# Attention of a two-block transformer kernel as a pipeline of four steps in a written order, with sixteen convolution taps by the scalar engine and accumulating DMA

## The chip, the cores and the metric

The kernel runs on one core of a Trainium2 chip. The metric is the device time of one execution in microseconds (us), as the median of several runs. Engines are named as in the profile: PE is TensorE (matmul), PEld its weight loads, DVE the vector engine, ACT the scalar engine, POOL GpSimd, SP the sync engine, which issues most of the DMA.

## What is computed

Two blocks follow each other over 512 tokens of width 1024. The change lies in the second, whose mixer (in the reference) is

```python
h = rms_norm(x, norm1_g)
q, k, v, glu_a, glu_b = split(h @ w_in)        # 512 wide each, q, k, v in 8 heads of 64
q, k = rms_norm(q, q_norm_g), rms_norm(k, k_norm_g)     # per head
attn = stick_breaking_attention(q, k, v)

c = glu_a * sigmoid(glu_b)
c = causal_depthwise_conv(c, conv_dw_w) + conv_dw_b     # 31 taps, 512 channels
c = silu(layer_norm(c, conv_ln_g, conv_ln_b))
x = x + concat([attn, c]) @ w_out
```

and whose attention is, for each head, over strictly earlier tokens s < t:

```python
z = q @ k.T / sqrt(64)
log_beta, log_one_minus = log_sigmoid(z), log_sigmoid(-z)
tail[t, s] = sum of log_one_minus[t, j] over s < j < t
out = exp(log_beta + tail) @ v
```

A feed-forward layer with a three-tap convolution follows.

## The kernel before

Matmuls in fp32 accuracy are made of three in a reduced format: each operand is split into a hi and a lo part, and hi x hi, lo x hi and hi x lo are summed in PSUM (L127 to L129). Weights come from memory as units of 1 MB (`raw`) and are split on the way: the hi part `whi` by an ACT cast (L199), the lo part `wlo` by a DVE subtraction (L205), or, for some units of the second block, by an ACT pass (L202) and an accumulating DMA that POOL issues (L203).

In the second block the mixer goes in this order. `glu(i)` makes one of four 128-channel chunks of the gated product (L707). `heads` makes q, then k: for each of four token tiles a projection, an ACT square (L742), a DVE sum (L744), three POOL operations (L745 to L747) and a DVE product (L748), then transposes and a split (L144). `conv` issues the taps of the depthwise convolution: 30 taps of each chunk as a DVE scalar_tensor_tensor (L851) and one as an ACT activation with the bias. The list `TURNS` (L835) says which chunk is next. `project` makes the values (copied out of PSUM at L132).

Attention has 12 steps: four pairs of heads (hp), and three groups n of key blocks, of width `WIDE` 384, 384 and 512 for each of two heads. `sticks(hp, n)` (L775) makes the logits (L785) and the mask (L790) in a pair of PSUM banks, then the absolute value (L794 on ACT or L797 on DVE), exp and log (ACT L799, L800), the running total's summands (DVE L801), and splits them into hi (ACT copy L135) and lo (DVE L136). `breaks(hp, n)` (L804) adds the sums of the later keys on top of the logits by matmuls with fixed triangles of minus one (L814, L817) and takes the exponential, the weights, on ACT (L819). `gather(hp)` (L822) multiplies them with the values (L829) into a single bank and splits the result into the place of q.

PSUM has pairs of banks, of which three are free to attention at a time, and two single banks. `conv_norm` (L884) normalizes the convolution over channels: mean by matmuls with ones (L889), subtraction (L893), squares and their sums (L897), scale (L902 to L915), Silu (L917) and a split. `attended` (L949) multiplies the gathered heads with the output weights (`half_out`), scales the residual (L954) and adds (L957); the same is then done for the convolution's half.

Which instruction comes when on each engine is settled by a scheduler that models time, under the constraints of data and buffers; `tc.issue_after(x)` adds that an instruction is to come behind x on its engine. Before the change only the taps are bound so, through `tap` (L837).

Of the kernel before, what the change touches and what calls it, by code (L numbers as in the profile page):

```python
# [79 lines left out]
def block_kernel(  # L80
# [22 lines left out]
    def pair():  # L103
        return psp.tile([P, 2, 512], F32, tag="pp", name="pp")
# [663 lines left out]
    def cols_of(a):  # L768

        at = 256 if a == 3 else 0  # L770
        return slice(at, at + T - a * P)

    zs = {}

    def sticks(hp, n):  # L775

        w = WIDE[n]
        zt = pair()
        z = zt[:, :, :w]

        for i, (ks, qs) in enumerate(((kT[0], qT[0]), (kT[0], qT[1]), (kT[1], qT[0]))):
            for a in STEPS[n]:
                for e in range(2):
                    hs = slice(e * HD, (e + 1) * HD)
                    pe.matmul(z[:, e, cols_of(a)], ks[hs, hp, a * P : (a + 1) * P],  # L785
                              qs[hs, hp, a * P :], start=i == 0 and a < 3, stop=False,
                              skip_group_check=True)
        for a in STEPS[n]:
            for e in range(2):
                pe.matmul(z[:, e, cols_of(a)][:, :P], identr, never, start=False, stop=False,  # L790
                          skip_group_check=True)
        ex = v3(t4(), 2, w)
        if hp < 2:
            act.activation(ex, z, AF.Abs)  # L794
        else:

            dve.tensor_scalar(ex.bitcast(I32), z.bitcast(I32), 0x7FFFFFFF, None,  # L797
                              ALU.bitwise_and)
        act.activation(ex, ex, AF.Exp, scale=-1.0)  # L799
        act.activation(ex, ex, AF.Ln, bias=1.0)  # L800
        dve.scalar_tensor_tensor(ex, z, 0.0, ex, ALU.max, ALU.add)  # L801
        zs[hp, n] = z
        return copy_split(*blk(hp, n), ex)

    def breaks(hp, n):

        w = WIDE[n]
        z = zs.pop((hp, n))
        for e in range(2):
            for a in STEPS[n]:  # L810
                out = z[:, e, cols_of(a)]
                for b in range(a + 1, 4):
                    for s in blk(hp, 0 if b > 1 else 1):
                        pe.matmul(out[:, (b - a) * P :], negone, s[:, e, cols_of(b)], start=False,  # L814
                                  stop=False, skip_group_check=True)
                for i, s in enumerate(blk(hp, n)):
                    pe.matmul(out, negtri, s[:, e, cols_of(a)], start=False, stop=i == 1,  # L817
                              skip_group_check=True)
        return act.activation(taken(hp, n), z, AF.Exp)  # L819

    def gather(hp):

        o = single(0)
        for n in range(3):
            for a in reversed(STEPS[n]):
                for e in range(2):
                    hs = slice(e * HD, (e + 1) * HD)
                    vs = slice(hp * P + e * HD, hp * P + (e + 1) * HD)
                    pe.matmul(o[hs, a * P :], v2[:, a, vs], taken(hp, n)[:, e, cols_of(a)],  # L829
                              start=a == 3, stop=a == 0, skip_group_check=True)  # L830
        return copy_split(qT[0][:, hp, :], qT[1][:, hp, :], o)

    TURNS = [0] * 8 + [0, 1] * 22 + [1, 2] * 8 + [2, 3] * 22 + [3] * 8  # L835
    done = [0] * 4
    tap = None  # L837

# [14 lines left out]
                    ALU.mult, ALU.add)  # L853

    norm2 = half("D1", 4, T, F32)
    conv(8, glu(0))
    split_early(2)
    conv(16, glu(1))
    qT = heads("G", "qg", HD ** -0.5, (0, 4, 4, 8), lambda: conv(8, glu(2)), early[:2])
    kT = heads("F", "kg", 1.0, (0, 6, 5, 8), lambda: conv(12, glu(3)), early[2:])  # L860
    v2 = half("E0", 4, T, F32)
    stk = {}

    def place(i):
        if i not in stk:
            name = ("D0", "B0", "D1", "C0", "C1", "B1", "E1")[i]
            stk[i] = slot(name, F32R if i < 4 else F32)
        return stk[i]

    def blk(hp, n):  # L870

        tl = place((hp % 2, 2, 3)[n])
        return tuple(part(tl, 2, WIDE[n], 2 * WIDE[n] * i) for i in range(2))

    def taken(hp, n):

        at = (0, 1024 * (hp % 2), 768)[n]
        return part(place(6 if n == 1 else 4 + hp % 2), 2, WIDE[n], at)

    cl = None  # L880
    ch = []
# [89 lines left out]
    seq = [(hp, n) for hp in range(4) for n in range(3)]  # L971
# [144 lines left out]
```

## Time and profile before

| | |
|---|---|
| median of 3 runs | 1244.39 us (1243.74 to 1244.77) |
| profiled execution | 1245.94 us |
| its span | 1244.2 us |
| granted PE clock, mean of the span | 0.995 |
| PE busy | 1230.3 us, 5712 matmuls |
| DVE busy | 754.0 us |
| ACT busy | 495.0 us |
| POOL busy | 113.5 us |
| DMA | 126.71 MB, 102 GB/s in the mean |

An execution's own time is a little longer than the span between its first and last instruction. Busy times leave out waiting and the issuing of DMAs. In a timeline a row is a run of like instructions: start, time from the first start to the last end, engine, line, operation, output and input tile, count, and, in brackets, how long the engine had been idle before it and what ended that. Instructions on one engine overlap at their ends, so that the spacing of starts is shorter than the time of one. The line numbers are those of the kernel before.

### The profile page before, as it was taken

The numbers are of one execution on the slowest core, as the hardware profiler recorded it, in microseconds if no ns is written. First come the engines' busy times: TensorE is split into PE (matmuls) and PEld (weight loads), VectorE is DVE, ScalarE is ACT, GpSimd is POOL, SyncE is SP. The second block draws the span as 40 slices with busy tenths as digits, with TensorE's granted clock in tenths as the row PEclk, the third lists the DMA queues.
The fourth block names the chain that finished last, engine by engine and source line by source line (L and its number), as shares of the span: only waits on it lengthen the run. The fifth ranks groups of instructions, "written<-read, shape, count | busy, mean of one in ns | idle before, by whom it ended". The sixth has DMA issues, their size and how long they took to land.

```text
span 1244.2 us, 13667 instructions
## 1 busy us (share of the span) xinstructions
PE 1230.3 (99%) x5712; PEld 1014.1 (82%) x5712; DVE 754.0 (61%) x823; ACT 495.0 (40%) x534; POOL 113.5 (9%) x137
## 2 busy tenths in 40 slices
PE   9999999999999999999999999999999999999998
PEld 7889888788888888888888887667888888888887
DVE  7855634744766674466373899877575555346532
ACT  6433424623544342243255338764343333123310
POOL 1100210012000000000053440000400000000000
PEclk9999999999999999999999999899999999999999
DMA  7223222312222222222346254301322222222222
GB/s 274 101 104 132 102 102 68 136 68 98 73 100 102 102 102 102 88 85 99 119 152 169 68 130 104 106 1 68 102 102 82 89 100 102 102 102 102 84 70 83
DMA packets 21597, 126.71 MB, mean 102 GB/s; under 512 B 2336, under 2 KB 4256, under 8 KB 7840
## 3 DMA queue, kind: packets, MB, share of 16 engines
q1 hardware_dynamic: 20096, 117.20, 26.7%
q0 software_dynamic: 1152, 8.39, 3.5%
q8 instruction: 44, 0.72, 0.2%
q10 hardware_dynamic: 288, 0.26, 0.1%
q14 instruction: 17, 0.14, 0.0%
HBM read 115.35 MB, written 2.10 MB: 94 GB/s over the span
## 4 chain that ended last, share of the span: by engine, by line
PE 90%; DVE 4%; POOL 2%; ACT 2%; issue 1%; DMA 1%; SPq 0%; DVEq 0%; POOLq 0%; ACTq 0%
PE pp L129 27%; PE pp L127 27%; PE pp L128 27%; DVE H L851 2%; PE ps L128 1%; PE ps L129 1%; PE ps L127 1%; POOL col L746 1%; PE pp L814 1%; PE pp L817 1%; PE ps L829 1%; DMA wlo<-raw 1%; POOL col L745 1%; PE pp L785 0%; PE ps L326 0%
## 5 line engine op out<-in xcount | busy, mean ns | idle before, releaser
L199 ACT CAST whi<-raw 128x2048 fp32r<-128x2048 f32 (+3 forms) x109 | 197.9, 1817 | 415.5 <-PE pp L128 335.7
L129 PE MATMUL pp<-B,wlo 128*128 128x512 f32 x672 | 262.5, 391 | 0.2
L127 PE MATMUL pp<-B,whi 128*128 128x512 f32 x672 | 261.7, 390 | 0.8 <-ACT whi L199 0.7
L128 PE MATMUL pp<-C,whi 128*128 128x512 f32 x672 | 262.2, 390 | 0.0
L205 DVE TENSOR_TENSOR wlo<-raw,whi 128x2048 fp32r<-128x2048 f32 (+3 forms) x101 | 219.3, 2172 | 66.1 <-ACT whi L199 65.6
L128 PE MATMUL pp<-G,whi 128*128 128x512 f32 x448 | 175.0, 391 | 0.0
L129 PE MATMUL pp<-F,wlo 128*128 128x512 f32 x416 | 162.2, 390 | 0.0
L127 PE MATMUL pp<-F,whi 128*128 128x512 f32 x416 | 161.5, 389 | 0.0
L129 PEld LDWEIGHTS pp<-B,wlo 128*128 128x128 f32 x672 | 126.1, 188 | 28.2 <-DVE wlo L205 1.5
L127 PEld LDWEIGHTS pp<-B,whi 128*128 128x128 f32 x672 | 126.3, 188 | 28.0 <-ACT whi L199 1.7
L128 PEld LDWEIGHTS pp<-C,whi 128*128 128x128 f32 x672 | 126.2, 188 | 26.8 <-issue 0.5
L128 PEld LDWEIGHTS pp<-G,whi 128*128 128x128 f32 x448 | 84.1, 188 | 17.5 <-issue 0.2
L655 DVE SCALAR_TENSOR_TENSOR H<-H,sm,H 128x512 f32<-128x512 f32 x132 | 92.8, 746 | 0.7
L634 DVE TENSOR_TENSOR A<-pp,A 128x1024 f32<-128x1024 f32 x23 | 28.2, 1224 | 105.5 <-PE pp L129 105.5
L129 PEld LDWEIGHTS pp<-F,wlo 128*128 128x128 f32 x416 | 78.1, 188 | 16.5 <-issue 0.2
L127 PEld LDWEIGHTS pp<-F,whi 128*128 128x128 f32 x416 | 78.1, 188 | 16.4 <-issue 0.2
L851 DVE SCALAR_TENSOR_TENSOR H<-H,sm,H 128x512 f32<-128x512 f32 x120 | 83.2, 742 | 2.7 <-ACT H L132 2.5
L660 DVE TENSOR_TENSOR H<-pp,rb 128x1024 f32<-128x1024 f32 x22 | 26.8, 1224 | 50.6 <-PE pp L129 44.4
L132 ACT ACTIVATE H<-H,sm 128x512 f32<-128x512 f32 x70 | 54.3, 808 | 4.6 <-DVE H L707 4.6
L1010 DVE TENSOR_TENSOR H<-pp,rb 128x512 f32<-128x512 f32 x22 | 15.2, 691 | 60.4 <-PE pp L129 55.3
L127 PE MATMUL pp<-D,whi 128*128 128x512 f32 x112 | 43.6, 389 | 0.0
L128 PE MATMUL pp<-E,whi 128*128 128x512 f32 x112 | 43.6, 389 | 0.0
(315 smaller groups left out, 1826.3 us busy)
## 6 DMA issues: line engine op xcount, KB each, us to landing
raw<-in_wts SPq DMA_DIRECT2D x99, 1024.0 KB, 4.8
wlo<-raw POOLq DMA_DIRECT2D x8, 1024.0 KB, 7.0
raw<-in_wts SPq DMA_DIRECT2D x8, 768.0 KB, 4.2
A<-in_xT SPq DMA_DIRECT2D x3, 512.0 KB, 6.7
out<-A SPq DMA_DIRECT2D x3, 512.0 KB, 2.8
D<-in_memT SPq DMA_DIRECT2D x1, 1024.0 KB, 11.4
raw<-in_wts SPq DMA_DIRECT2D x3, 256.0 KB, 7.6
A<-in_xT SPq DMA_DIRECT2D x2, 256.0 KB, 3.9
```

Of the source, the lines that this page charges most:

```text
L127: pe.matmul(out, wh, xh, start=start, stop=False, **kw)
L128: pe.matmul(out, wh, xl, start=False, stop=False, **kw)
L129: pe.matmul(out, wl, xh, start=False, stop=stop, **kw)
L132: act.activation(out, in_, AF.Identity, scale=scale, bias=bias)
L199: act.copy(hi[:, cs], raw[:, cs])
L205: dve.tensor_tensor(lo[:, cs], raw[:, cs], hi[:, cs].bitcast(F32), ALU.subtract)
L634: dve.tensor_tensor(hu, pt, hu, ALU.add)
L655: dve.scalar_tensor_tensor(dst, hs[:, k : k + 512], w(k), dst, ALU.mult, ALU.add)
L660: dve.tensor_tensor(hs[:, :, 2:], pt, over2(rb), ALU.mult)
L745: pool.tensor_scalar(ms, ms, rr2[:, t : t + 1], EPS, ALU.mult, ALU.add)
L851: tap = dve.scalar_tensor_tensor(cv[:, i, :], cc[:, i, k : k + 512], par("dw_w", 4 * k + i), cv[:, i, :], ALU.mult, ALU.add)
L1010: dve.tensor_tensor(hs[:, 2:514], pt[:, 0, :], rb, ALU.mult)
```

## The change

Attention becomes a class `Step` with one object for each of the 12 steps, k = 3 hp + n. `put` binds every instruction of a step behind the one that was written before it for the same engine, so that the order on PE, ACT and DVE in the attention is the written one, taps included. Steps run four deep: logits(k+4), absolute(k+4), logs and total(k+3) and split(k+2) are issued around breaks(k). Steps with k % 4 == 3 use the two single banks, the others pairs. The gather writes into its own step's bank. The absolute value is on ACT for k < 4. The places of the split totals and of the weights in SBUF change.

Taps 22 to 29 of chunks 0 and 1, sixteen in all, are made on ACT as a scaled copy, and summed by 14 accumulating DMAs from POOL (256 KB each), each issued behind the power chain of a q or k tile; one DVE add puts the sum on top. `TURNS` has the other 104 taps. The core of the diff:

```diff
@@ heads
-            pool.tensor_scalar(ms, ms, rr[:, t : t + 1], None, ALU.mult)
+            power = pool.tensor_scalar(ms, ms, rr[:, t : t + 1], None, ALU.mult)
             conv(taps[t], dve.tensor_tensor(heads8, ...))
+            by_dma(power)
@@ attention
+    order = {}
+    def put(eng, op, *args, **kw):
+        with tc.issue_after(order[eng].ins) if eng in order else nullcontext():
+            order[eng] = op(*args, **kw)
+        return order[eng]
...
+        def logits(self):
+            hp, n, w = self.hp, self.n, self.w
+            if self.k % 4 < 3:
+                zt = pair()
+                self.z = [zt[:, e, :w] for e in range(2)]
+                self.all = [(slice(0, 2), zt[:, :, :w])]
+                self.bank = zt[:, 0, :]
+            else:
+                zt = [single(e) for e in range(2)]
+                self.z = [tl[:, :w] for tl in zt]
+                self.all = list(enumerate(self.z))
+                self.bank = zt[0]
...
+        def gather(self):
+            hp = self.hp
+            for n in range(3):
+                for a in reversed(STEPS[n]):
...
+                        put("pe", pe.matmul, self.bank[hs, a * P :], v2[:, a, vs],
+                            taken(hp, n)[:, e, cols_of(a)], start=a == 3, stop=a == 0,
+                            skip_group_check=True)
+        def keep(self):
+            hi, lo = qT[0][:, self.hp, :], qT[1][:, self.hp, :]
+            put("act", act.copy, hi, self.bank)
+            return put("dve", dve.tensor_tensor, lo, self.bank, hi.bitcast(F32), ALU.subtract)
@@ taps
-    TURNS = [0] * 8 + [0, 1] * 22 + [1, 2] * 8 + [2, 3] * 22 + [3] * 8
+    TURNS = [0] * 8 + [0, 1] * 14 + [1] * 8 + [2] * 26 + [2, 3] * 4 + [3] * 26
+    sums = half("D0", 4, T, F32)
+    aside = list(range(22, 30))
+    def by_dma(behind):
+        k = aside.pop(0)
+        for i in range(2):
+            out = sums[:, i, :] if k == 22 else sums[:, 2 + i, :]
+            act.activation(out, cc[:, i, k : k + 512], AF.Copy, scale=par("dw_w", 4 * k + i))
+            if k > 22:
+                with tc.issue_after(behind.ins):
+                    pool.dma_start(out=sums[:, i, :], in_=out, accum_op=ALU.add)
...
     v2 = half("E0", 4, T, F32)
+    dve.tensor_tensor(cv[:, 0:2, :], cv[:, 0:2, :], sums[:, 0:2, :], ALU.add)
@@ the loop
-    conv(10, sticks(*seq[0]))
-    conv(14, sticks(*seq[1]))
+    for k, n in ((0, 10), (1, 14)):
+        st = steps[k]
+        st.logits()
+        st.absolute()
+        st.logs()
+        st.total()
+        st.split()
+        taps_here(n)
     project()
-    todo = 2
-    for i, x in enumerate(seq):
-        while todo < len(seq) and todo <= i + 2 and not (x[1] == 2 and seq[todo][1] == 1):
-            conv(2, sticks(*seq[todo]))
-            todo += 1
-        weighted = breaks(*x)
-        if x[1] == 2:
-            gathered = gather(x[0])
+    for st in steps[2:4]:
+        st.logits()
+        st.absolute()
+    steps[2].logs()
+    steps[2].total()
+    for k, st in enumerate(steps):
+        a, b, c = (steps[k + i] if k + i < 12 else None for i in (4, 3, 2))
+        st.breaks()
+        weighted = st.weigh()
+        if b:
+            b.logs()
+        if st.n == 2:
+            st.gather()
+            gathered = st.keep()
+        if a:
+            a.logits()
+            a.absolute()
+        if b:
+            b.total()
+        if c:
+            c.split()
+        if TURNS:
+            taps_here(1 if k < 9 else 4)
```

`taps_here(n)` issues n taps behind the last DVE instruction of the chain.

The order of instructions at three places follows; L779 is `put` in the change, D_, B_ and C_ are places of split totals and weights, G_ and F_ the hi and lo parts of q and k, E_ weights or values, t_ work tiles, pp pairs and ps singles of PSUM, H_2138 the convolution's result, A_76 and A_77 the residual.

DVE at the entry of the attention, before. L801 is the total, the last of them here that of step 2:

```order
L707 TENSOR_TENSOR H_2137<-t_5003 128x512
L851 SCALAR_TENSOR_TENSOR H_2138<-H_2137,sm,H_2138 128x512 x10
L801 SCALAR_TENSOR_TENSOR t_5061<-pp,t_5061 128x768
L851 SCALAR_TENSOR_TENSOR H_2138<-H_2137,sm,H_2138 128x512
L801 SCALAR_TENSOR_TENSOR t_5088<-pp,t_5088 128x768
L851 SCALAR_TENSOR_TENSOR H_2138<-H_2137,sm,H_2138 128x512
L136 TENSOR_TENSOR D_5066<-t_5061,D_5066 128x768
L851 SCALAR_TENSOR_TENSOR H_2138<-H_2137,sm,H_2138 128x512 x2
L136 TENSOR_TENSOR D_5093<-t_5088,D_5093 128x768
L851 SCALAR_TENSOR_TENSOR H_2138<-H_2137,sm,H_2138 128x512 x2
L801 SCALAR_TENSOR_TENSOR t_5237<-pp,t_5237 128x1024
```

Between the product of L707 and total(2) there were 16 taps, in five groups. And now, on the same engine and from the same product; L779 with pp is total(0), total(1) and total(2) in turn, with D_ split(0) and split(1), L893 is the tap:

```order
L707 TENSOR_TENSOR H_2137<-t_5034 128x512
L893 SCALAR_TENSOR_TENSOR H_2138<-H_2137,sm,H_2138 128x512
L144 SCALAR_TENSOR_TENSOR F_4814<-pp,col_4804,F_4813 128x4x256
L893 SCALAR_TENSOR_TENSOR H_2138<-H_2137,sm,H_2138 128x512 x11
L779 SCALAR_TENSOR_TENSOR t_5093<-pp,t_5093 128x768
L893 SCALAR_TENSOR_TENSOR H_2138<-H_2137,sm,H_2138 128x512 x3
L779 TENSOR_TENSOR D_5098<-t_5093,D_5098 128x768
L893 SCALAR_TENSOR_TENSOR H_2138<-H_2137,sm,H_2138 128x512 x12
L779 SCALAR_TENSOR_TENSOR t_5120<-pp,t_5120 128x768
L779 TENSOR_TENSOR D_5125<-t_5120,D_5125 128x768
L893 SCALAR_TENSOR_TENSOR H_2138<-H_2137,sm,H_2138 128x512 x14
L779 SCALAR_TENSOR_TENSOR t_5269<-pp,t_5269 128x1024
```

Total(2) stood behind 10, 1, 1, 2 and 2 taps after the product of L707; it now stands behind 1, 11, 3, 12 and 14.

PE just behind the value projection, before (breaks(0), then breaks(1) and breaks(2)):

```order
L817 MATMUL pp<-D_5066,negtri 128x128 x2
L814 MATMUL pp<-D_5066,negone 128x256 x2
L814 MATMUL pp<-D_5066,negone 128x128 x2
L817 MATMUL pp<-D_5093,negtri 128x384 x2
L814 MATMUL pp<-D_5066,negone 128x256 x2
L814 MATMUL pp<-D_5066,negone 128x128 x2
L817 MATMUL pp<-D_5093,negtri 128x384 x2
L814 MATMUL pp<-D_5093,negone 128x384 x2
L814 MATMUL pp<-D_5066,negone 128x256 x2
L814 MATMUL pp<-D_5066,negone 128x128 x2
L889 MATMUL ps_5651<-H_2138,ones 128x512 x2
```

The breaks of the first three steps followed each other with no logits between. And now, on PE from the end of breaks(0):

```order
L779 MATMUL pp<-D_5098,negtri 128x128 x2
L779 MATMUL pp<-G_4553,F_4813 128x384 x2
L779 MATMUL pp<-G_4554,F_4813 128x384 x2
L779 MATMUL pp<-G_4553,F_4814 128x384 x2
L779 MATMUL pp<-never,identr 128x128 x2
L779 MATMUL pp<-D_5098,negone 128x256 x2
L779 MATMUL pp<-D_5098,negone 128x128 x2
L779 MATMUL pp<-D_5125,negtri 128x384 x2
L779 MATMUL pp<-D_5098,negone 128x256 x2
L779 MATMUL pp<-D_5098,negone 128x128 x2
L779 MATMUL pp<-D_5125,negtri 128x384 x2
L779 MATMUL pp<-G_4553,F_4813 128x512 x2
```

The logits of step 4 (384 wide) and of step 5 (512 wide) stand between breaks(0) and breaks(1) and between breaks(1) and breaks(2), in the PSUM pairs of steps 0 and 1.

DVE behind the last gather, before (L136 is the split of that gather, L893 the subtraction of the convolution's mean):

```order
L893 SCALAR_TENSOR_TENSOR H_2138<-ps_5651,H_2138 128x512 x4
L897 TENSOR_TENSOR t_5657<-t_5657,t_5660 128x512
L897 TENSOR_TENSOR t_5657<-t_5657,acc 128x512 x2
L906 TENSOR_SCALAR col_5676<-ps_5671 128x4
L908 TENSOR_TENSOR t_5678<-ident,col_5679 128x512
L136 TENSOR_TENSOR G_4553<-ps_5639,G_4552 128x512
L954 TENSOR_TENSOR A_76<-A_76,rb 128x1024 x2
L954 TENSOR_TENSOR A_77<-A_77,rb 128x1024 x2
L915 TENSOR_TENSOR H_2138<-H_2138,ps_5682 128x512 x4
```

Before, the mean was subtracted ahead of the split. And now on DVE (the first row is the split of the last gather; L1010 and L1013 are the old L954 and L957, L949 the old L893, L953 the old L897):

```order
L779 TENSOR_TENSOR G_4554<-ps_5569,G_4553 128x512
L1010 TENSOR_TENSOR A_76<-A_76,rb 128x1024 x2
L1010 TENSOR_TENSOR A_77<-A_77,rb 128x1024 x2
L949 SCALAR_TENSOR_TENSOR H_2138<-ps_5675,H_2138 128x512 x4
L1013 SCALAR_TENSOR_TENSOR A_76<-A_76,sm,pp 128x512 x2
L953 TENSOR_TENSOR t_5681<-t_5681,t_5684 128x512
L1013 SCALAR_TENSOR_TENSOR A_76<-A_76,sm,pp 128x512 x2
L205 TENSOR_TENSOR wlo<-raw,whi 128x2048
L953 TENSOR_TENSOR t_5681<-t_5681,acc 128x512 x2
L962 TENSOR_SCALAR col_5700<-ps_5695 128x4
L964 TENSOR_TENSOR t_5702<-ident,col_5703 128x512
```

The subtraction of the mean stood ahead of the last gather's split; it now stands behind it and behind the four products on the residual.

## Rows read from the trace of the kernel before

**Rows 1.** The page, section 1: busy us, share of the span, instructions of each engine

```profile
PE 1230.3 (99%) x5712; PEld 1014.1 (82%) x5712; DVE 754.0 (61%) x823; ACT 495.0 (40%) x534; POOL 113.5 (9%) x137
```

**Rows 2.** Windows, PE: stretch, us, busy (count), granted clock, DMA share, GB/s

```profile
785.00:790.00 5.00, 3.27 (x21) 0.93 0.93 375
790.00:800.00 10.00, 9.62 (x45) 0.52 0.01 2
800.00:830.00 30.00, 26.38 (x164) 1.00 0.00 1
830.00:855.00 25.00, 24.35 (x114) 1.00 0.00 1
```

**Rows 3.** Timeline of DVE, taps and totals ahead of the attention

```profile
690.53 3.10 DVE L851 SCALAR_TENSOR_TENSOR H<-H,sm,H 128x512 f32<-128x512 f32 x4
...
696.50 2.73 DVE L851 SCALAR_TENSOR_TENSOR H<-H,sm,H 128x512 f32<-128x512 f32 x4
...
753.35 0.68 DVE L707 TENSOR_TENSOR H<-t 128x512 f32<-128x512 f32 x1
...
768.14 1.21 DVE L801 SCALAR_TENSOR_TENSOR t<-pp,t 128x1024 f32<-128x1024 f32 x1
```

**Rows 4.** Timeline of ACT around the entry

```profile
765.72 1.06 ACT L800 ACTIVATE t<-t 128x1024 f32<-128x1024 f32 x1
...
769.83 1.92 ACT L202 ACTIVATE wlo<-raw 128x2048 fp32r<-128x2048 f32 x1 [1.80 <-PE ps L128]
...
773.45 1.04 ACT L135 CAST C<-t 128x1024 fp32r<-128x1024 f32 x1
...
776.21 0.66 ACT L132 ACTIVATE E<-ps,rr 128x512 f32<-128x512 f32 x1
...
778.57 0.81 ACT L819 ACTIVATE C<-pp 128x768 f32<-128x768 f32 x1
...
784.93 0.59 ACT L135 CAST G<-ps 128x512 fp32r<-128x512 f32 x1 [0.89 <-PE ps L829]
```

**Rows 5.** Timeline of PE around the entry

```profile
772.35 0.39 PE L129 MATMUL ps<-whi,C 128*128 128x512 f32 x1
772.58 0.33 PE L814 MATMUL pp<-D,negone 128*128 128x128 f32 x2
...
773.89 0.63 PE L814 MATMUL pp<-D,negone 128*128 128x256 f32 x4
...
775.57 0.94 PE L814 MATMUL pp<-D,negone 128*128 128x384 f32 x6
...
779.94 0.91 PE L785 MATMUL pp<-G,F 64*128 64x256 f32 x12
...
781.37 0.87 PE L829 MATMUL ps<-C,E 128*64 128x128 f32 x8
```

**Rows 6.** Timeline of PE in the loop, two waits for ACT

```profile
808.55 0.91 PE L785 MATMUL pp<-G,F 64*128 64x256 f32 x12 [0.90 <-ACT C L819]
...
820.54 1.08 PE L829 MATMUL ps<-C,E 128*64 128x512 f32 x4 [1.55 <-ACT C L819]
```

**Rows 7.** Timeline of DVE at the tail

```profile
832.42 2.48 DVE L893 SCALAR_TENSOR_TENSOR H<-ps,H 128x512 f32<-128x512 f32 x4 [0.51 <-PE ps L889]
...
843.38 4.62 DVE L954 TENSOR_TENSOR A<-A,rb 128x1024 f32<-128x1024 f32 x4
...
850.31 2.71 DVE L957 SCALAR_TENSOR_TENSOR A<-A,sm,pp 128x512 f32<-128x512 f32 x4
852.95 2.28 DVE L205 TENSOR_TENSOR wlo<-raw,whi 128x2048 fp32r<-128x2048 f32 x1
```

**Rows 8.** Line L203 on POOL, ns of one; the page's DMA issues, KB, us to landing

```profile
L203 POOL DMA_DIRECT2D wlo<-raw x8: 838/920/1047, 656.1 to 776.6; - x8
...
DMA to landing us min/median/max: 6.9/7.0/8.9
...
out<-A SPq DMA_DIRECT2D x3, 512.0 KB, 2.8
```

More of the change, by code (lines that the diff above doesn't have):

```diff
@@ L771, in cols_of, with __init__ @@
         return slice(at, at + T - a * P)
[L773 to L781, printed above, removed]
+    order = {}
[3 more added lines that the diff above has]
+        return order[eng]
+    class Step:
+        def __init__(self, k):
+            self.k, self.hp, self.n = k, k // 3, k % 3
+            self.w = WIDE[self.n]
+        def logits(self):
[10 more added lines that the diff above has]
+                self.bank = zt[0]
+            for i, (ks, qs) in enumerate(((kT[0], qT[0]), (kT[0], qT[1]), (kT[1], qT[0]))):
+                for a in STEPS[n]:
+                    for e in range(2):
+                        hs = slice(e * HD, (e + 1) * HD)
+                        put("pe", pe.matmul, self.z[e][:, cols_of(a)],
+                            ks[hs, hp, a * P : (a + 1) * P], qs[hs, hp, a * P :],
+                            start=i == 0 and a < 3, stop=False, skip_group_check=True)
@@ L782, in sticks @@
             for a in STEPS[n]:
                 for e in range(2):
[L784 to L788, printed above, removed]
-            for e in range(2):
-                pe.matmul(z[:, e, cols_of(a)][:, :P], identr, never, start=False, stop=False,
-                          skip_group_check=True)
@@ L792, in sticks @@
[L792 to L831, printed above, removed]
@@ L835, in block_kernel, with absolute @@
-    TURNS = [0] * 8 + [0, 1] * 22 + [1, 2] * 8 + [2, 3] * 22 + [3] * 8
+                    put("pe", pe.matmul, self.z[e][:, cols_of(a)][:, :P], identr, never,
+                        start=False, stop=False, skip_group_check=True)
+        def absolute(self):
+            self.ex = v3(t4(), 2, self.w)
+            for e, z in self.all:
+                if self.k < 4:
+                    put("act", act.activation, self.ex[:, e], z, AF.Abs)
+                else:
+                    put("dve", dve.tensor_scalar, self.ex[:, e].bitcast(I32), z.bitcast(I32),
+                        0x7FFFFFFF, None, ALU.bitwise_and)
@@ new lines, in logs, with total, split @@
+        def logs(self):
+            put("act", act.activation, self.ex, self.ex, AF.Exp, scale=-1.0)
+            put("act", act.activation, self.ex, self.ex, AF.Ln, bias=1.0)
+        def total(self):
+            for e, z in self.all:
+                put("dve", dve.scalar_tensor_tensor, self.ex[:, e], z, 0.0, self.ex[:, e],
+                    ALU.max, ALU.add)
+        def split(self):
+            hi, lo = blk(self.hp, self.n)
+            put("act", act.copy, hi, self.ex)
+            return put("dve", dve.tensor_tensor, lo, self.ex, hi.bitcast(F32), ALU.subtract)
@@ new lines, in breaks @@
+        def breaks(self):
+            hp, n = self.hp, self.n
+            for e in range(2):
+                for a in STEPS[n]:
+                    out = self.z[e][:, cols_of(a)]
+                    for b in range(a + 1, 4):
+                        for s in blk(hp, 0 if b > 1 else 1):
+                            put("pe", pe.matmul, out[:, (b - a) * P :], negone,
+                                s[:, e, cols_of(b)], start=False, stop=False,
+                                skip_group_check=True)
+                    for i, s in enumerate(blk(hp, n)):
+                        put("pe", pe.matmul, out, negtri, s[:, e, cols_of(a)], start=False,
+                            stop=i == 1, skip_group_check=True)
@@ new lines, in weigh @@
+        def weigh(self):
+            for e, z in self.all:
+                last = put("act", act.activation, taken(self.hp, self.n)[:, e], z, AF.Exp)
+            return last
+        def gather(self):
+            hp = self.hp
+            for n in range(3):
+                for a in reversed(STEPS[n]):
+                    for e in range(2):
+                        hs = slice(e * HD, (e + 1) * HD)
+                        vs = slice(hp * P + e * HD, hp * P + (e + 1) * HD)
+                        put("pe", pe.matmul, self.bank[hs, a * P :], v2[:, a, vs],
+                            taken(hp, n)[:, e, cols_of(a)], start=a == 3, stop=a == 0,
+                            skip_group_check=True)
@@ L865, in place @@
         if i not in stk:
-            name = ("D0", "B0", "D1", "C0", "C1", "B1", "E1")[i]
-            stk[i] = slot(name, F32R if i < 4 else F32)
+            name = ("D1", "B0", "D0", "B1", "C0", "C1", "E1")[i]
+            stk[i] = slot(name, F32R if i < 5 else F32)
         return stk[i]
     def blk(hp, n):
-        tl = place((hp % 2, 2, 3)[n])
+        tl = place((hp % 2, 2 + hp % 2, 4)[n])
         return tuple(part(tl, 2, WIDE[n], 2 * WIDE[n] * i) for i in range(2))
     def taken(hp, n):
-        at = (0, 1024 * (hp % 2), 768)[n]
-        return part(place(6 if n == 1 else 4 + hp % 2), 2, WIDE[n], at)
+        i, at = ((5 + hp % 2, 0), (6, 768), (5, 768))[n]
+        return part(place(i), 2, WIDE[n], at)
     cl = None
@@ L969, in project, with taps_here @@
             identity(v2[:, t, :], ps, scale=rr[:, t : t + 1])
-    seq = [(hp, n) for hp in range(4) for n in range(3)]
-    conv(10, sticks(*seq[0]))
-    conv(14, sticks(*seq[1]))
-    project()
-    todo = 2
-    for i, x in enumerate(seq):
-        while todo < len(seq) and todo <= i + 2 and not (x[1] == 2 and seq[todo][1] == 1):
-            conv(2, sticks(*seq[todo]))
-            todo += 1
-        weighted = breaks(*x)
-        if x[1] == 2:
-            gathered = gather(x[0])
+    steps = [Step(k) for k in range(12)]
+    def taps_here(n):
+        conv(n, order["dve"])
+        order["dve"] = tap
+    for k, n in ((0, 10), (1, 14)):
[6 more added lines that the diff above has]
+        taps_here(n)
+    project()
+    for st in steps[2:4]:
[21 more added lines that the diff above has]
+            taps_here(1 if k < 9 else 4)
     with tc.issue_after(weighted.ins):
```

## The prediction

> **What bounds the kernel now.** I read the busy shares first: TensorE (PE) is busy 99% of the span, the vector engine (DVE) 61%, the scalar engine (ACT) 40% [rows 1]. So the end is set by PE's work and by the gaps in it; work taken from DVE or ACT is worth nothing unless PE waited for it. Then I cut the attention stretch into windows [rows 2]. PE's gaps there are 5.00 − 3.27 = 1.73, 10.00 − 9.62 = 0.38, 30.00 − 26.38 = 3.62 and 25.00 − 24.35 = 0.65 us, together 6.4 us. The granted clock is 0.93 in the first window and 0.52 in the second, after those first gaps: that is the lower of PE's two levels (1.2 of 2.4 GHz) for nearly the whole window, and it cost about 9.62 x 0.48 + 3.27 x 0.07 = 4.8 us. The two together, **11.2 us, are all that a perfect order of the attention could give back**. PE's matmuls are the same before and after, so the forecast is a count of PE's waits: 11.2 us old ones against the new. Last I read each engine's timeline around 772 us, where the value projection ends and the attention loop begins (the entry), and around 842 us, where the last gather ends (the tail).
>
> **Taps moved off DVE.** Sixteen taps leave. A DVE tap that alternates between two tiles costs 2.73 / 4 = 0.68 by its group, 0.663 by spacing of starts; one that follows another on the same tile costs 3.10 / 4 = 0.775 [rows 3]. The saving is 16 x 0.663 = 10.6 us, less the one added add of some 0.7, less about 0.11 for every tap that the new order of chunks (26 twos in a row, 26 threes in a row) links to its predecessor: about 48 x 0.11 = 5.3. Some 4.6 us of DVE time are gained, on an engine that is busy 61% [rows 1]. The sixteen ACT passes are some 0.8 us each, 13 us on an engine with half its time free there: cost 0. POOL issues 14 accumulating DMAs at about 0.92 [rows 8], off PE's path: cost 0, the cover being the time until the single add behind the k heads. Landing time of a 256 KB accumulating transfer is not in the trace: 2.8 us (512 KB without accumulation) and 7.0 us (1 MB with it) [rows 8] bound it. I take 3.6, nearer the first since it is a quarter of the second's bytes: hidden. At 7.0 the chain of them could hold the add, and with it DVE, by up to 8 us; that end stays in the range.
>
> **The entry.** This term decides. Three things stand in fixed order now. PE: logits(3), breaks(0), logits(4), breaks(1), logits(5). Since logits(4) takes the PSUM pair of step 0, it needs the weights' Exp of step 0, and logits(5) that of step 1, which stands on ACT behind the hi copy of step 2, and that behind total(2) on DVE. PE gets there at 772.6, when the value projection ends [rows 5].
> - DVE: the gated product of chunk 3 ends at about 754 [rows 3]; behind it the change has 27 taps (18 linked x 0.775 + 9 x 0.663 = 19.9), the k heads' split (1.2) and total(0), split(0), total(1) at about 0.87 (384 columns a head against 1.21 for 512 [rows 3]): total(1) is done at 754 + 23.7 = 777.7.
> - ACT: four weight casts run from 769.83, two in 773.45 − 769.83 = 3.62 us, with the values' copy-out among them [rows 4]: free at 777.63. So copy(1) ends at 778.5 and split(1) at 779.4.
> - DVE then has 14 taps (10.7) ahead of total(2): 779.4 + 10.7 + 1.2 = 791.3. Copy(2) takes 1.04 and the Exp of step 1 0.81 [rows 4]: logits(5) may start at **793.2**. In the trace before, total(2) runs at 768.14, ahead of most of these taps [rows 3]. That is the step that moves: 14 taps now stand in front of an operation for which ACT, and through it PE, waits.
> - PE work meanwhile: logits(3) 781.37 − 779.94 = 1.43, breaks(0) 773.89 − 772.58 = 1.31, breaks(1) 775.57 − 773.89 = 1.68 [rows 5], logits(4) about 1.0 (six columns of 384 in place of twelve shorter matmuls): 5.4 us. New wait 793.2 − 772.6 − 5.4 = **15.2 us**, in three gaps: about 3.3 (logits(3) behind the copy-out that frees the single banks), 4.5 (logits(4)) and 7.4 (logits(5)).
>
> The row shows 3.10 us for four linked taps and 2.73 for four alternating ones [rows 3], so a dependence on the instruction just before costs 0.11 us. The Trainium skill (VectorE: DVE Perf Modes, section "The DRAIN you can't avoid") has it otherwise: a semaphore between successive operations costs nothing extra, since the pipe is drained in any case. By that rule total(2) would come with 30 linked taps at 0.663, some 3.4 us earlier on DVE alone; copy(1) would still wait for ACT, so logits(5) would start at about 791.7 and the sum would be 1.5 us less. The measurement decides, and I keep 0.775.
>
> **The loop.** After the entry each logits(k+4) follows breaks(k) and needs the Exp between them. The trace has one such wait: 0.90 us in front of an L785 group, released by ACT's L819 [rows 6]. For k = 3, 4, 6, 7 that is 3.6 us. For k = 2, 5, 8 the gather writes the very bank that this Exp reads, so it waits too: 1.55 was seen for a gather behind an Exp [rows 6], 0.9 is the least, and I take 1.1: 3.3. Behind the gathers at k = 2 and 5 logits(k+4) need the bank emptied: copy 0.59 [rows 4], subtract some 0.68, hand-over, 1.35 each: 2.7. **9.6, say 10 us.** Nothing stands on PE between that could cover it; before, the sums L889 and the other order did. Bounds: 0, if the scalar engine runs a step ahead, to 16, if every wait is 1.55.
>
> **The tail.** The convolution's mean needs a single bank, and step 11 holds both until its last Exp. So its four matmuls stand behind gather(11), where before they were spread over the loop and the subtraction L893 began at 832.42, ahead of the last gather [rows 7]. DVE's order is now: subtract of keep, four products of L1010 (4.62), the four subtractions (2.48), the first adds of L1013 (2.71), a weight's lo part 2.28 [rows 7] and three sums of squares (about 2.0), 15.4 with the 1.3 of the copy ahead. PE's cover is the mean's matmuls (1.8) and 23 products at 0.23 (772.35 to 772.58 [rows 5]): 7.0. Wait 8.4, and about 1 more where the first convolution product waits for the scale and the Silu: **9.4 us.** Bounds: 3, if the rotation of DVE's order lets the four subtractions pass, to 12.
>
> **Clock.** Two of the new groups of gaps, entry and tail, are longer than the 2.1 us of gaps after which the trace shows 0.52 [rows 2]. Each should cost what the one cost, 4.8: two come (9.6), the old one goes.
>
> **Sum.** New waits 15.2 + 10 + 9.4 = 34.6; old waits −6.4; clock 9.6 − 4.8 = +4.8. Together +33.0 on the profiled execution's 1245.94 us: 1278.9. That execution stands 1.5 us over the median of the runs, 1244.39, so the median forecast is **1277**.
>
> **Rivals.**
> - *Half clock in the loop as well* (0.13): gaps of one to two us come every 4 us from k = 2 on. For it: the old fall followed gaps of just this size. Against: 800 to 830 had 3.62 us of gaps in 30 and kept 1.00 [rows 2]. Price: three more episodes, +14: 1291.
> - *The accumulating DMAs land late* (0.10): at 7.0 us each the last taps' sum holds the add at the head of DVE's attention work: +8, 1285.
> - *Half the price* (0.12): the taps or casts at the entry run earlier than counted and the loop's waits overlap with one another: entry 8, loop 5, tail 5, one clock episode: 18 − 6.4 = +11.6: 1256.
> - *Faster* (0.10): with four steps in flight each operand is ready when PE comes to it. DVE reaches the 14 taps so early that total(2) is done by 778, 13 us ahead of my count; the entry then costs only the 3.3 of the copy-out, and the clock never falls. With 2 us of tail: 5.3 − 11.2 = −5.9, 1238.5. It decides from the point where all new waits with their clock are under 11.2 us. For it: 16 taps are off DVE before the entry. Against: ACT is bound by its casts until 777.6 whatever DVE does, and the taps stand ahead of total(2) in a written order.
> - *No change* (0.05): new waits equal the relief, or the moved taps and steps were never on PE's path, and the gaps are merely relocated: 1244.
>
> **How the numbers follow.** The forecast case has 0.50. Slower by more than 0.2% (2.5 us, about what a measurement of this kernel can tell from no change) hold the forecast, the first three rivals: 0.85; faster 0.10, same 0.05. The forecast case alone, with the bounds of loop and tail (−10 to +6, and −6 to +3, not all together), runs from 1264 to 1284. The range goes down to 1252, which takes in half the price, and up to 1297, which takes in the half clock; outside lie about 0.17 below and a few hundredths above.
>
> **What would show it.** Right: a PE gap of over 5 us ending at an L785-like logits group released by ACT's Exp around 790; a second window of granted clock near 0.5 behind it; 0.9 to 1.5 us in front of each logits group in the loop, released by the Exp; and a gap of some 8 us behind the last gather, released by the sums of squares. Wrong: total(2) done before 780, PE windows with gaps under 11 us in all, a mean that starts ahead of the last gather, or a wait of DVE for a transfer in front of the new add.

## The result and the profile after

| | before | changed |
|---|---|---|
| median | 1244.45 us (4 runs, 1243.74 to 1244.77) | 1285.84 us (4 runs, 1280.97 to 1286.17) |
| ratio | | 1.0324, 95% interval 1.0299 to 1.0349 |
| profiled execution, its span | 1245.94 us, 1244.2 us | 1280.97 us, 1279.3 us |
| granted clock of the span | 0.995 | 0.982 |

The change is slower by 3.2%; the forecast was 1277, in a range from 1252 to 1297. The profiled execution is the shortest of the four; the other three, at a granted clock of 0.977, are 5 us longer, about what one more fall of the clock costs, so times inside the trace are held against 1280.97 and medians against 1285.84.

The page's busy times, as [rows 1], say that PE did the same number of matmuls, with 97% of a longer span:

```profile
PE 1239.1 (97%) x5712; PEld 1021.5 (80%) x5712; DVE 752.6 (59%) x815; ACT 505.2 (39%) x552; POOL 125.0 (10%) x151
```

PE's windows, which answer to [rows 2], with the same columns; the stretches are the value projection, the entry, two pieces of the loop, its end with the products of the gathered heads, and the tail:

```profile
745.00:770.00 25.00, 19.62 (x86) 0.80 0.71 174
780.00:810.00 30.00, 18.22 (x97) 0.72 0.54 140
810.00:830.00 20.00, 14.95 (x112) 1.00 0.01 2
830.00:840.00 10.00, 8.94 (x44) 0.66 0.00 0
840.00:870.00 30.00, 28.89 (x152) 1.00 0.00 1
870.00:890.00 20.00, 13.90 (x48) 0.74 0.15 52
```

The reader is to see two things in each row: the gap (length less busy) and the clock. The gaps are 5.4, 11.8, 5.1, 1.1, 1.1 and 6.1, together 30.5 us. The clock cost 19.62 x 0.20 = 3.9, 18.22 x 0.28 = 5.1, 8.94 x 0.34 = 3.0 and 13.90 x 0.26 = 3.6: 15.6 us. That is 46.1 us in place of the old 11.2, or 34.9 more; the spans differ by 35.1. Nearly the whole loss is therefore in PE's waits between 745 and 890 and in the clock that fell after them.

What PE waited for between 640 and 900 (total, times, longest):

```profile
PE pp L779 <- ACT C L779: 7.6, 5, 3.3
PE pp L779 <- ACT E L779: 6.3, 2, 5.4
PE ps L958 <- DVE t L953: 6.1, 1, 6.1
PE ps L128 <- DMA wlo<-raw: 5.0, 2, 3.0
PE pp L779 <- DVE G L779: 2.8, 2, 1.4
PE ps L779 <- ACT E L132: 2.0, 1, 2.0
```

And where, in PE's timeline (in brackets the idle time before the row, and what ended it; L779 is `put`):

```profile
749.15 0.80 PE L128 MATMUL ps<-wlo,B 128*128 128x512 f32 x1 [2.00 <-DMA wlo<-raw]
...
760.12 0.79 PE L128 MATMUL ps<-wlo,B 128*128 128x512 f32 x1 [3.04 <-DMA wlo<-raw]
...
784.28 0.90 PE L779 MATMUL ps<-G,F 64*128 64x256 f32 x12 [1.98 <-ACT E L132]
...
791.21 1.33 PE L779 MATMUL pp<-G,F 64*128 64x384 f32 x6 [3.32 <-ACT C L779]
...
801.62 1.65 PE L779 MATMUL pp<-G,F 64*128 64x512 f32 x6 [5.37 <-ACT E L779]
...
819.88 0.96 PE L779 MATMUL pp<-G,F 64*128 64x512 f32 x6 [0.90 <-ACT E L779]
...
824.92 1.52 PE L779 MATMUL pp<-E,E 128*64 128x128 f32 x12 [1.11 <-ACT C L779]
...
828.71 0.91 PE L779 MATMUL pp<-G,F 64*128 64x256 f32 x12 [1.41 <-DVE G L779]
...
877.35 1.87 PE L958 MATMUL ps<-ones,t 128*128 128x1 f32 x8 [6.10 <-DVE t L953]
```

The rows at 784, 791 and 801 are logits(3), logits(4) and logits(5): the three gaps of the entry that were forecast, ended by the releasers that were named. Those at 819 to 828 are the loop's pattern: a weights' Exp, a gather behind its Exp, a bank that is emptied. The row at 877 is the tail. The first two rows were not forecast: PE waits for the lo parts of the value weights. POOL's timeline in front of them shows why (L909 issues the taps' DMAs, L203 the weights'):

```profile
738.98 1.84 POOL L909 DMA_DIRECT2D D<-D  x2 [0.15 <-issue]
740.29 1.41 POOL L203 DMA_DIRECT2D wlo<-raw  x1
...
745.15 1.85 POOL L909 DMA_DIRECT2D D<-D  x2 [0.17 <-issue]
748.62 0.86 POOL L203 DMA_DIRECT2D wlo<-raw  x1 [1.62 <-ACT wlo L202]
```

In the kernel before, the same two units were issued at

```profile
735.86 0.93 POOL L203 DMA_DIRECT2D wlo<-raw  x1 [0.53 <-ACT wlo L202]
...
748.60 0.94 POOL L203 DMA_DIRECT2D wlo<-raw  x1 [6.04 <-ACT wlo L202]
```

In the change each is issued behind a pair of tap transfers, but only the first is issued later than before, by 4.4 us: ACT makes its lo pass (L202) at 738.09 in place of 733.64, behind tap passes that waited for their own transfers. The second is issued at the same time as before, 748.62 for 748.60, so all its delay lies behind the issue. Landing, for the line L203, and on the page for both kinds:

```profile
DMA to landing us min/median/max: 6.9/7.8/11.5
...
wlo<-raw POOLq DMA_DIRECT2D x8, 1024.0 KB, 7.8
...
D<-D POOLq DMA_DIRECT2D x14, 256.0 KB, 3.8
```

The slowest weight unit took 11.5 us (the second of the two), where before the slowest took 8.9 and the median was 7.0 [rows 8].

### The profile page after: what moved, and what is told of

Same layout as the page of the kernel before. It is cut to its first block, busy times and chain, and to the rows that moved or that the text cites. A ratio compares the mean times of both kernels' runs of the same rounds, so it can differ in the third digit from the quotient of the medians.

```text
span 1279.3 us, 13713 instructions
## 1 busy us (share of the span) xinstructions
PE 1239.1 (97%) x5712; PEld 1021.5 (80%) x5712; DVE 752.6 (59%) x815; ACT 505.2 (39%) x552; POOL 125.0 (10%) x151
## 4 chain that ended last, share of the span: by engine, by line
PE 93%; DVE 2%; ACT 2%; DMA 1%; issue 1%; SPq 0%; DVEq 0%; ACTq 0%
PE pp L128 28%; PE pp L129 28%; PE pp L127 28%; PE pp L779 3%; PE ps L128 2%; PE ps L129 2%; PE ps L127 2%; PE ps L779 1%; DMA wlo<-raw 1%; DVE H L893 1%; PE ps L326 0%; ACT whi L199 0%; ACT C L779 0%; DMA A<-in_xT 0%; PE ps L345 0%
## 5 line engine op out<-in xcount | busy, mean ns | idle before, releaser
L655 DVE SCALAR_TENSOR_TENSOR H<-H,sm,H 128x512 f32<-128x512 f32 x132 | 92.8, 747 | 0.7
L893 DVE SCALAR_TENSOR_TENSOR H<-H,sm,H 128x512 f32<-128x512 f32 x104 | 75.8, 748 | 4.3 <-ACT H L132 2.5
L1090 DVE TENSOR_TENSOR H<-pp,rb 128x512 f32<-128x512 f32 x22 | 15.2, 691 | 61.0 <-PE pp L129 54.9
```

Source lines behind the costliest of these rows:

```text
L655: dve.scalar_tensor_tensor(dst, hs[:, k : k + 512], w(k), dst, ALU.mult, ALU.add)
L893: tap = dve.scalar_tensor_tensor(cv[:, i, :], cc[:, i, k : k + 512], par("dw_w", 4 * k + i), cv[:, i, :], ALU.mult, ALU.add)
L1090: dve.tensor_tensor(hs[:, 2:514], pt[:, 0, :], rb, ALU.mult)
```

## The experiments

All times are medians; before ran beside them at 1245.1 to 1245.2. The theory is that of the prediction with one cause added: waits from the written order (entry, loop), from the mean behind the last gather (tail), and from weights that land late (value projection), each with the clock that falls behind it. The rivals are that one of these is the whole cause, or that four steps in flight cost by themselves.

| run | edit | us | ratio to before |
|---|---|---|---|
| e1 | pipeline alone, taps as before | 1269.31 | 1.0182 (1.0154 to 1.0210) |
| e2 | taps alone, old attention | 1254.00 | 1.0062 (1.0044 to 1.0081) |
| e3 | ten tap DMAs | 1276.24 | 1.0250 (1.0233 to 1.0267) |
| e4 | 3 taps ahead of total(2) | 1275.55 | 1.0235 (1.0209 to 1.0261) |
| e5 | mean in a pair | 1270.81 | 1.0198 (1.0182 to 1.0215) |
| e6 | steps in free order | 1265.19 | 1.0158 (1.0142 to 1.0173) |
| e7 | old attention, ten tap DMAs | 1250.89 | 1.0047 (1.0031 to 1.0064) |
| e8 | old attention, six tap DMAs | 1242.27 | 0.9978 (0.9969 to 0.9988) |
| e9 | free order, mean in a pair, six tap DMAs | 1243.36 | 0.9986 (0.9977 to 0.9996) |
| e10 | written order, else mended | 1266.19 | 1.0151 (1.0109 to 1.0194) |
| e11 | no accumulation | 1273.70 | 1.0230 (1.0203 to 1.0257) |
| e12 | e8 with linked taps | 1247.82 | 1.0021 (1.0012 to 1.0030) |

**The two halves of the change, each alone.** e1 takes the taps' part out of the change; e2 puts it into the kernel before.

```diff
# e1, on the changed kernel
-            by_dma(power)
...
-    TURNS = [0] * 8 + [0, 1] * 14 + [1] * 8 + [2] * 26 + [2, 3] * 4 + [3] * 26
+    TURNS = [0] * 8 + [0, 1] * 22 + [1, 2] * 8 + [2, 3] * 22 + [3] * 8
... (sums, aside and by_dma go)
-    dve.tensor_tensor(cv[:, 0:2, :], cv[:, 0:2, :], sums[:, 0:2, :], ALU.add)
# e2: by_dma, its calls, the add and the new TURNS on the kernel before
```

> The pipeline of steps with all 120 taps on DVE again, in the old order of chunks, and no accumulating DMA for taps. If the written order sets most of the loss (order theory), only the value projection's part goes, some 10 us of waits and half clock between 745 and 770 in the changed kernel's trace (5.4 + 4.4), and the entry gets worse, since the same taps stand ahead of total(2) and DVE has 16 more: 1270 to 1284. If the taps' DMAs set the loss (DMA theory), all but the old waits go: 1244 to 1255.

> The old attention and its free order, with the sixteen taps on ACT and the 14 accumulating DMAs. Order theory: only the wait of the value projection for weights comes in (5.4 of gaps and up to 4.4 of clock), less what DVE's relief gives back in the attention, at most the old 11.3: 1244 to 1256. DMA theory: 1270 or more.

Both halves cost: 24 us the pipeline, 9 us the taps, 33 together. The change costs 41, so some 8 come only from the two together. e2's time is inside what was expected; e1's is just under it. The new PE waits of e2 are those for the weights:

```profile
PE ps L128 <- DMA wlo<-raw: 5.6, 2, 3.7
```

In e1 no such wait is left, and the tail's 6.1 and the loop's 0.9, 1.1 and 1.4 are unchanged. That the entry would be worse in e1 was wrong: it waits 4.87 + 0.92 + 0.90, 6.7 us in place of 10.7. In the change PE's order has the first eight matmuls of logits(0) ahead of two tiles of the value projection and the rest behind them; the second late weight unit (760.12 above) stands between. ACT's first Abs comes behind that, and DVE stands 4.43 us in front of total(0). The changed kernel's timelines of PE, ACT and DVE:

```profile
756.40 0.68 PE L779 MATMUL pp<-G,F 64*128 64x256 f32 x8
...
767.92 0.44 PE L779 MATMUL pp<-G,F 64*128 64x256 f32 x4
```

```profile
768.99 0.81 ACT L779 ACTIVATE t<-pp 128x768 f32<-128x768 f32 x1 [0.27 <-PE pp L779]
```

```profile
771.59 0.96 DVE L779 SCALAR_TENSOR_TENSOR t<-pp,t 128x768 f32<-128x768 f32 x1 [4.43 <-ACT t L779]
...
787.66 10.98 DVE L893 SCALAR_TENSOR_TENSOR H<-H,sm,H 128x512 f32<-128x512 f32 x14
798.56 1.22 DVE L779 SCALAR_TENSOR_TENSOR t<-pp,t 128x1024 f32<-128x1024 f32 x1
```

In e1 logits(0) run in one piece, from 751.74. Its DVE has total(0) at 758.17, and total(2) 14 us earlier than the change, with cheaper taps ahead of it:

```profile
758.17 0.95 DVE L778 SCALAR_TENSOR_TENSOR t<-pp,t 128x768 f32<-128x768 f32 x1
...
775.34 9.36 DVE L892 SCALAR_TENSOR_TENSOR H<-H,sm,H 128x512 f32<-128x512 f32 x14
784.62 1.22 DVE L778 SCALAR_TENSOR_TENSOR t<-pp,t 128x1024 f32<-128x1024 f32 x1
```

The late start of logits(0) is not what makes the change's entry longer, though. e11 (below) has the change's order of chunks without the late weights; its logits(0) start at 751.98 and its total(0) at 757.28, as early as in e1, and yet its entry waits 11.2 us. Its DVE and PE:

```profile
775.22 0.95 DVE L779 SCALAR_TENSOR_TENSOR t<-pp,t 128x768 f32<-128x768 f32 x1
...
790.47 1.22 DVE L779 SCALAR_TENSOR_TENSOR t<-pp,t 128x1024 f32<-128x1024 f32 x1
```

```profile
776.19 1.28 PE L779 MATMUL ps<-G,F 64*128 64x256 f32 x12 [3.23 <-ACT E L132]
...
783.13 1.33 PE L779 MATMUL pp<-G,F 64*128 64x384 f32 x6 [2.06 <-ACT C L779]
...
793.53 1.65 PE L779 MATMUL pp<-G,F 64*128 64x512 f32 x6 [5.95 <-ACT E L779]
```

From the product L707 on, e11 and the change have 27 taps ahead of total(1), most of them linked; e1 has 22, which alternate. So total(1) comes at 775.22 in e11 and at 769.85 in e1, and copy(1) stands on ACT behind four weight casts there (777.84) and behind two here (773.61). That the order of chunks is the cause is a reading of these rows: no run changes it alone in the written pipeline.

**The late weights.** e3 has two pairs of tap transfers fewer; e11 has all the ACT passes and no accumulation.

```diff
# e3 (e7 and e8 likewise, from 24 and from 26; TURNS takes the taps that come back)
-    aside = list(range(22, 30))
+    aside = list(range(24, 30))
     def by_dma(behind):
+        if not aside:
+            return
...
# e11
-            if k > 22:
-                with tc.issue_after(behind.ins):
-                    pool.dma_start(out=sums[:, i, :], in_=out, accum_op=ALU.add)
```

> The change with four of the sixteen taps back on DVE: ten accumulating DMAs, none behind the last two k tiles. If the four last DMAs, 738.98 to 745.15 on POOL, delay the two weight units of the value projection (5.0 us of PE's waits for DMA), these land about 7 us after their issue again, the waits and their half clock go, and the time falls by 5 to 10: 1275 to 1281. If the weights wait for something else (the raw loads, or the bandwidth shared with them), nothing changes: 1284 to 1288.

> The change with the 14 accumulating DMAs left out: the sixteen ACT passes and the add remain, but only tap 22 of the two chunks is in the sum, so the output lacks 14 taps. If the DMAs delay the weights, and with them the values' copy-out and the attention's first ACT work, PE's 5.0 us wait and the clock behind it go, and DVE's 4.4 us wait for total(0) too: 1268 to 1277. If it is ACT's passes, 1284 to 1288.

Both came as the theory has it, 9.6 and 12.1 us faster. In e3 one wait of 1.05 for a weight unit is left of 5.0, with a new one of 1.64 for the last k tile's product (L748); in e11 neither. PE's windows from 740 to 760, of the change and of e11:

```profile
740.00:760.00 20.00, 14.74 (x71) 0.89 0.99 210
```

```profile
740.00:760.00 20.00, 19.64 (x109) 1.00 0.66 178
```

So the accumulating transfers, not ACT's passes by themselves, hold up the weights: with them the 16 DMA engines are busy 0.99 of this window, without them 0.66. For the first unit part of the way is seen: the passes wait for their transfers, and the unit's L202 stands behind them. Whether the second waits behind the tap transfers in the same queue or for busy DMA engines stays open; no run parts the two.

**The entry.** e4 moves eleven taps from in front of total(2) into the loop.

```diff
-    for k, n in ((0, 10), (1, 14)):
+    for k, n in ((0, 10), (1, 3)):
```

> The change with 3 taps in place of 14 ahead of total(2); the other 11 go into the loop, one a step. Order theory: 11 x 0.775 = 8.5 us less ahead of total(2), so the wait of logits(5), 5.37, goes, and the half clock behind it (1.7 to 2.3): 1277 to 1281. If ACT's casts or the PSUM buffers bound the entry instead, logits(5) waits as before or PE waits later in the loop, where a tap a step is added: 1284 to 1288.

10.3 us faster, a little more than expected, although PE waited longer for the weights in the profiled execution (7.9 us, in the change 5.0). logits(5), where PE stood 5.37 us, now has this row:

```profile
797.19 0.98 PE L779 MATMUL pp<-G,F 64*128 64x512 f32 x6 [0.90 <-ACT E L779]
```

0.90 is the loop's own price. The taps in the loop cost no new wait.

**The tail.** e5 puts the convolution's mean into a pair of banks.

```diff
-        mu = single(1)
+        mu = pair()[:, 0, :]
```

> The change with the convolution's mean in a PSUM pair in place of the single bank that step 11 holds; so its four matmuls no longer stand behind the last gather. Order theory: the wait of 6.10 for the sums of squares goes, most of the 3.8 of half clock with it: 1275 to 1280. If the length of the chain behind the mean sets the wait, or the products wait for the pair instead, 1283 to 1287.

No PE wait is left behind the last gather, and the time is below the expected 1275: 15.0 us of medians. The two profiled executions differ by 9.5, as expected; the rest is that the other runs of the change had a lower clock than the profiled one (0.977 against 0.982), and those of e5 0.985 to 0.991.

**The written order.** e6 takes the binding out of `put` and leaves all else.

```diff
-        with tc.issue_after(order[eng].ins) if eng in order else nullcontext():
-            order[eng] = op(*args, **kw)
+        order[eng] = op(*args, **kw)
```

> The change without the binding of put: the same steps, banks, depth and taps, but the scheduler orders PE, ACT and DVE within them (taps stay behind the split that they stood behind). If the written order costs (order theory), breaks(1) no longer stands behind logits(4), the entry's gaps of 10.7 fall by 3 to 8 and the loop's 0.9 to 1.4 shrink in part: 1262 to 1277. If the sharing of banks by four steps in flight costs, whatever the order, 1281 to 1288.

20.7 us faster, with the same banks, depth and taps. PE's waits in entry and loop shrink to 0.78, 1.59, 0.31, 1.62 and 0.48; those of the weights (5.7) and the tail (6.1) stay, since nothing was done about them. e9 mends these two as well; e10 mends everything but the order, with 3 taps ahead of total(2) and two a step in the loop. Both have eight taps on ACT (`range(26, 30)`) and the mean in a pair; the cut shows what is new in them.

```diff
# e9 and e10
+    TURNS = [0] * 10 + [0, 1] * 16 + [1, 2] * 10 + [2] * 6 + [2, 3] * 14 + [3] * 16
...
# e10
-            taps_here(1 if k < 9 else 4)
+            taps_here(2 if k < 9 else 4)
```

> The pipeline of steps in the scheduler's order, with the mean in a pair and six accumulating DMAs (eight taps) behind q tiles only. If the loss is the sum of the four places found (weights late, written order at the entry, in the loop, mean behind the last gather), what is left are waits like those of the free order in the attention, 4 to 6 us, with at most one fall of the clock: 1239 to 1246. If four steps in flight cost by themselves, 1250 or more.

> The written order kept, with the mean in a pair, six accumulating DMAs, and 3 taps ahead of total(2), two a step in the loop. Order theory: the loop's waits (8.3 us) and some 5 at the entry stay, as written, with 2.5 to 7 of half clock, where before has 11.3: 1249 to 1256. If the loop's waits were only a consequence of the late start, 1244 to 1248; if two taps a step hold the breaks, 1257 or more.

e9 came as expected, with one wait of note left in the attention:

```profile
788.61 0.51 PE L778 MATMUL ps<-B,negone 128*128 128x128 f32 x2 [2.78 <-ACT B L778]
```

Four steps in flight cost little by themselves: against e8 below, the old attention with the same taps, e9 is 1.1 us slower, and the two intervals overlap. In e10 the profiled execution is at 1254.93, inside what was expected, but the median is 11 us above, and that part is a miss. Its windows:

```profile
745.00:770.00 25.00, 23.41 (x122) 1.00 0.43 123
770.00:795.00 25.00, 17.77 (x95) 0.80 0.65 168
795.00:830.00 35.00, 27.83 (x201) 1.00 0.01 1
830.00:870.00 40.00, 38.63 (x181) 1.00 0.08 27
```

The gaps are 1.6, 7.2, 7.2 and 1.4, with 3.6 of clock: 20.9 us against the old 11.2, which is its 9.7 us over before. The other three executions have the same program at a granted clock of 0.983 to 0.985 in place of 0.996; where it fell in them no trace shows. The loop's gaps of about 1 us left the clock at 1.00 in this execution (795 to 870), while in the profiled one of the change it was 0.66 between 830 and 840. The expectation had room for one more fall; at the forecast's 4.8 each, 11 us are the price of about two.

**The taps with the old attention.** e7 and e8 stop at ten and at six transfers. e7 has the change's order of chunks, with long rows of linked taps; e8 mixes the chunks. e12 is e8 with the order of chunks of the change.

> The old attention with twelve taps on ACT and ten accumulating DMAs, none behind the last two k tiles. If the taps alone cost by the two weight units of the value projection that land late (5.6 us of waits and some 3.9 of half clock), these go, and DVE's relief may give back up to 5 in the attention: 1240 to 1248. If they cost in another way (ACT's passes in front of the squares, the linked taps), 1250 to 1255 as with fourteen.

> The old attention with eight taps on ACT and six accumulating DMAs, all behind q tiles, and chunks mixed in the order of taps as far as they can be. Same theory: no wait for a weight unit at all, attention waits like those with the taps alone (5 to 6 us against 11.3 with clock before): 1239 to 1245. Otherwise 1246 to 1252.

> The old attention with six accumulating DMAs, but the order of chunks of the change (26 twos in a row, 26 threes), about 36 more taps linked to their predecessor at 0.11 us: 4 us of DVE time more ahead of the attention's first totals. If linked taps cost, 1 to 4 us slower than with mixed chunks (1242.3): 1243 to 1247. If a dependence on the instruction before costs nothing, the same 1241 to 1243.

e7, at 1250.89, falls into the second of its cases: no wait for weights is left, but PE waits 1.65 us for the last k tile's product L748 and 0.95 for the split behind it, so the taps also hold up the heads. In the changed kernel, between 680 and 750, ACT shows what may do it, a wait of each new pass for the transfer that empties its buffer:

```profile
ACT D L906 <- DMA D<-D: 22.6, 10, 7.6
```

The squares of the k tiles stand in that queue. In e7 the same wait is 18.8 us in all, 6 times, the longest 7.5. e8, which has no transfer behind a k tile, waits neither for the weights nor for L748 (and 0.64 for the split), and **beats both kernels: 0.9978 of before**, 2.8 us. e12 is 5.5 us slower than e8, more than expected. The linked taps are not shown as the reason at the entry, though: total(2) is earlier there than in e8, and the added waits lie at the tail (2.55 us for L974, 0.71 for a copy). Part may be the clock: e12 was granted 0.993 to 0.996, e8 0.997 to 1.000. The order of chunks costs here; by which path stays open. It also means that not all of the step from e7 to e8 is due to the fewer transfers: e12, with six transfers and linked taps, is 2.6 us slower than before.

## Why the prediction was right

- **Entry.** 15.2 us forecast, 10.7 measured (1.98 + 3.32 + 5.37, for 3.3, 4.5 and 7.4), at the places and with the releasers named. The step "DVE then has 14 taps ahead of total(2)" is shown by e4, the fixed order by e6. The path was sized well: in e11, where no weights are late, total(1) and total(2) are done at 776.2 and 791.7 and logits(5) start at 793.5, for the forecast 777.7, 791.3 and 793.2. In the change the late weights moved all of it: PE came to logits(3) at 782.3 for 772.6 and to logits(5) at 801.6, 19.3 us later, for the forecast 20.6. What was mis-sized is PE's work between: 8.65 us for 5.4 (9.3 in e11), since the clock had fallen (0.72 from 780 to 810). A PE that works slower ahead of a wait for ACT only shortens that wait; the forecast took the wait at full clock and added 4.8 for the fall, and so counted part of it twice.
- **Linked taps.** The 14 linked ones took 10.98 us (forecast 10.7), and e1's 14 alternating ones 9.36. The Trainium skill (VectorE: DVE Perf Modes, section "The DRAIN you can't avoid") would have them equal, since by it a semaphore between successive operations costs nothing extra. The trace does not agree: 1.62 us over 14 taps, 0.12 each, and the measurement decides.
- **Loop.** 9.6 to 10 forecast; 8.3 measured, at 0.90, 1.11 and 1.41 for the forecast 0.9, 1.1 and 1.35. Only logits(7) and logits(11), the steps in the single banks, waited less (0.21 and 0.16).
- **Tail.** 8.4 + 1 forecast, 6.10 + 0.84 measured; e5 shows the cause. PE had more to do meanwhile than the 7.0 us counted: it began the mean at 862.08 and stopped 9.2 us later, the mean alone taking 3.1 for the 1.8 counted.
- **Accumulating transfers: the step that failed.** "POOL issues 14 accumulating DMAs ... off PE's path: cost 0". Their landing was well put (3.8, forecast 3.6), and the wait of DVE for a transfer in front of the add, which was on the list of what would show the forecast wrong, came but is only 0.71. What was missed is who else uses POOL's DMA: the weight units of the value projection, 5.0 us of PE's waits, 9.3 with the small gap and the clock in that window. Missed with it is that ACT's passes, priced at 0 as well, wait 22.6 us for these transfers, with a weight's lo pass behind them. The rule to count every instruction that shares a queue was applied to DVE and ACT, not to POOL's transfers.
- **Clock.** Two falls were forecast (9.6), 15.6 us were measured: two short ones at the value projection, behind the two waits for weights, the rest at the entry, in the loop and in the tail. The rival of a half clock in the loop came true once in the profiled execution, where three more falls were priced.
- **Sum.** New gaps 30.5 against 34.6 forecast, clock 15.6 against 9.6: 46.1 against 44.2. The tail's 0.84 lies behind 890 and is not in the 30.5. The profiled execution was forecast at 1278.9 and measured 1280.97, but that nearness is in part luck: a term set to zero (5.4 of gaps) and more clock made up for an entry, loop and tail that were 8.7 too dear. The median is 9 us above its forecast of 1277, since in the other executions the clock was lower still (0.977). The faster rival's point, all new waits under 11.2 us, was missed by 35.

## What to carry to other kernels

A written order is only as good as its slowest assumption: one in-order queue that holds a filler (taps, copy-outs) ahead of an operation for which another engine waits turns that filler into a wait; here the scheduler's order of the same steps was 21 us cheaper. Before an accumulating transfer is called free, list what else the same engine issues as DMA and when that must land, and which engine waits for its buffers: with the old attention fourteen transfers were a loss of 9 us, six placed early with mixed chunks a gain of 3, and six with linked taps a loss of 3. Price a gap on PE with the clock behind it: here the falls added half of what the gaps cost.

## What the runs showed that was not expected

- The same program loses the clock a different number of times: the change was granted 0.982 in one execution and 0.977 in three (5 us apart), e10 0.996 in one and 0.983 to 0.985 in three (11 us apart). e8 and e9, with 4 to 6 us of gaps between 640 and 900, stayed within 3.1 us in ten runs each.
- A 256 KB accumulating transfer landed in 3.3 to 6.1 us, median 3.8. A 1 MB one took up to 11.5 with those around it, 13.1 in e4, e5 and e6 and 13.2 in e2, against 6.9 at the least.
- The second weight unit was issued at the same time as before (748.62 for 748.60) and still made PE wait 3.04 us.
